# Both MLP products of a hybrid encoder layer as seven block products of halves, with the blocks of u kept in DRAM

## The chip, the cores and the metric

One Trainium2 chip; the kernel runs on one of its cores. The metric is the device time of one launch in microseconds (us). Three runs of the kernel before are shown; their median is 2542.11 us.

## The reference, cut to what matters

One encoder layer over 1024 tokens of 1024 channels in float32: a token mixer of three branches, then an MLP. The change is in the MLP alone (between the norms, D_MODEL = 1024, D_FF = 4096):

```python
def squared_relu_mlp(h, w_up, w_down):
    return jnp.square(jax.nn.relu(h @ w_up)) @ w_down
# out = x1 + rmsnorm(squared_relu_mlp(rmsnorm(x1) * ln_mlp_pre, w_up, w_down)) * ln_mlp_post
```

## The kernel before

The parts follow one another: the input norm, the projections and mixers, the out projection (`out_proj`, from L1037), the MLP (`mlp`, from L1124). A scheduler orders the instructions of all engines by their priority, which is the order in the code; `high_priority` moves loads and casts ahead by a number of instructions, and every wait is put in by it. Tiles come from pools with a fixed number of buffers; a tile waits until the one that had its place is given back.

Every large product is made of three matmuls. An operand is split into hi (rounded to the format that TensorE takes in one pass, an ACT cast, L160) and lo (the rest, a DVE subtraction, L161); `product` (L183 to L190) adds the stationary hi with the moving hi (L188), the stationary hi with the moving lo (L189), and the stationary lo with the moving hi (L190), for every slice k of 128 of the contracted dimension. Each matmul has 128 x 128 stationary and up to 512 moving columns and adds into one bank (128 x 512) of PSUM.

In `out_proj` the 8 token tiles are lifted, multiplied (24 matmuls for each of two banks), normed, and turned by transposes into h (`h_hi`, `h_lo`: channels on the partitions, all 1024 tokens). Its weights, 8 pairs of hi and lo tiles, are held to the end; 12 of those 16 tiles are in the pool `w` of 15 tiles of 128 x 1024, from which the MLP takes its weights too.

The MLP works in 16 blocks of 256 hidden channels. `ups` (L1133) makes u = relu(h w_up)^2 of a block, for each half of the tokens and each 128 channels: 8 slices x 3 matmuls into a bank, relu on ACT (L1142), the square on DVE (L1143), and the split into `uh` and `ul`. `downs` (L1156) multiplies the u of a block with its rows of w_down: 8 token tiles x 2 halves of the output channels, 6 matmuls each, and adds the bank into `acc` in SBUF on DVE (L1164). The order is ups(b+1), then downs(b). The last two blocks are taken together by `finish` (L1166), which also norms a token tile (L1175 to L1182), adds x1 and stores it (L1183). Weights are loaded by the SP queue (L174), 512 KB each. GpSimd (POOL) does a few memsets in the mixers and issues no transfer.

```python
def product(self, bank, stat, mov, close=True, opened=False):            # L183
    for k in range(n):
        (sh, sl), (mh, ml) = stat[k], mov[k]
        mm(bank, sh, mh, start=(k == 0 and not opened), stop=False)      # L188
        mm(bank, sh, ml, start=False, stop=False)                        # L189
        mm(bank, sl, mh, start=False, stop=(close and k == n - 1))       # L190
```

Of the kernel before, what the change touches and what calls it, by code (L numbers as in the profile page):

```python
# [9 lines left out]
F32 = mybir.dt.float32  # L10
# [11 lines left out]
NK = 8  # L22
# [4 lines left out]
LEVELS = (0, 1, 2, 4, 8, 16)  # L27

# [32 lines left out]
def layout(inputs):  # L61
    """The inputs as the kernel reads them: moved, sliced, repeated or padded with zeros, never changed."""
    f = {k: np.asarray(v) for k, v in inputs.items()}
    w = f["w_in"][0]
# [18 lines left out]
    for n, h in enumerate(LEVELS[2:]):  # L83
# [14 lines left out]
        "wup": np.stack([tiled(f["w_up"][0][:, c:c + 256]) for c in range(0, 4096, 256)]),  # L98
        "wdown": np.stack([tiled(f["w_down"][0][c:c + 256]) for c in range(0, 4096, 256)]),
# [14 lines left out]
class Pipe:  # L114
    """What all the parts share: the pools, the constants, the ways to project and to normalise."""

    def __init__(self, ctx, tc, a, out):
        self.tc, self.nc, self.a, self.out = tc, tc.nc, a, out
        pool = lambda name, bufs=1, **k: ctx.enter_context(tc.tile_pool(name=name, bufs=bufs, **k))
        self.const = pool("const")  # L120
        self.hp = pool("h")
        self.wp = pool("w", 15)
        self.dram = pool("scratch", space=DRAM)
        self.pj = pool("pj", 5, space=PSUM)
        self.mx = pool("mx", 3, space=PSUM)
        self.n = 0
        self.ahead = 300
        self.evac = 80
# [29 lines left out]
    def split(self, raw, hi, lo):  # L158
        """raw = hi + lo exactly, both in the format that the tensor engine takes in one pass."""
# [3 lines left out]
    def load_w(self, src, nk, width, late=None):  # L163
        """src [P, nk, width] in DRAM; returns for every k the pair (hi, lo) of [P, width] views."""
# [17 lines left out]
    def product(self, bank, stat, mov, close=True, opened=False):  # L182
        """bank += sum over k of stat[k].T @ mov[k], each a (hi, lo) pair."""  # L183
        mm = self.nc.tensor.matmul
        n = len(stat)
        for k in range(n):
            (sh, sl), (mh, ml) = stat[k], mov[k]
            mm(bank, sh, mh, start=(k == 0 and not opened), stop=False)  # L188
            mm(bank, sh, ml, start=False, stop=False)  # L189
            mm(bank, sl, mh, start=False, stop=(close and k == n - 1))  # L190
# [17 lines left out]
    def rstd(self, ms, eps):  # L208
        """(ms + eps) ** -0.5 for ms, eps [P, 1]: a square root and a reciprocal, and a Newton step on them."""
# [35 lines left out]
def lower_bound(p):  # L245
    """lb = clip(cumsum(softmax(logits, axis=0))[0] - cumsum(...)[0], 0, 1) over the one layer there is."""
# [13 lines left out]
def stage_in(p):  # L260
    """hT = rmsnorm(x) transposed, split: [P, k, T]. A generator: two token tiles a step."""
# [62 lines left out]
def small_part(p):  # L324
    """The 32 narrow columns, B's decay and C's per-token scalars."""
# [91 lines left out]
def conv_silu(p, bank, ct, prev, s):  # L417
    """silu of the causal conv over time of one channel tile, half a sequence; returns (out, padded input)."""
# [15 lines left out]
def keys_part(p, w, pair):  # L434
    """C's keys of two heads: k to DRAM, k k^T with its decay to DRAM, |k|^2."""
# [27 lines left out]
def solve_part(p):  # L463
    """Inverses of the 64 x 64 unit triangles on the diagonal, one per partition (half a, head, chunk).
    A generator: the steps lie between other work."""
# [3 lines left out]
    def turn(x, dst):  # L469
        """x [(a, n), 64] -> dst [(a, m), 64] with dst[a, m, n] = x[a, n, m]."""  # L470
# [162 lines left out]
def decay_part(p, w, pair):  # L633
    """A's decay f = lb + (1 - lb) sigmoid(z) and key k = (1 - lb) sigmoid(-z) of two heads, to DRAM."""
# [66 lines left out]
def token_pairs(p, w):  # L701
    """h @ w (256 columns) two token tiles at a time: yields (t, bank [P, 2, 256])."""
# [7 lines left out]
def first_project(p, w, ready):  # L710
    """A's values of the first group and the 32 narrow columns, tile by tile as the tokens come."""
# [16 lines left out]
def v_project(p, w):  # L728
    """A's or B's values of a group, [tokens, 256], four token tiles per slot."""
# [24 lines left out]
def delta_rule(p, st, q, vv, h, half, o_out, ss_out, sq_out):  # L754
    """One head of C, 512 tokens."""
# [281 lines left out]
def out_proj(p):  # L1037
    """x1 = x + rmsnorm(y @ w_out) * w, and h2 = rmsnorm(x1) * w transposed and split."""
# [12 lines left out]
    def lift(t):  # L1051
        """The tokens of tile t, all channels: transposed and split."""
# [71 lines left out]
def mlp(p, ctx):  # L1124
# [112 lines left out]
```

## Time and profile before

| | |
|---|---|
| runs shown, us | 2533.89, 2542.11, 2547.4 (median 2542.11) |
| span of the profiled execution, us | 2545.3 |
| first and last MLP matmul start, us | 1837.5 and 2537.5 |
| TensorE (PE), VectorE (DVE), ScalarE (ACT) busy | 99%, 55%, 31% |
| mean granted TensorE clock | 0.995 of 2.4 GHz |
| transfers | 200 MB, 79 GB/s in the mean |

The profile is of one execution. Its time beside the span is not given apart from the runs, so the span stands for it: 3.2 us above the median of the runs shown. Times in rows count from the span's start. PE is matmuls, PEld weight loads, which overlap them. A matmul record is longer than the time to the next one, since they are pipelined.

### The profile page before, as it was taken

How to read it: one execution, taken by the hardware profiler on the slowest of the kernel's cores; microseconds unless marked ns; L12 is line 12 of the kernel's file. 1: busy time of each engine (PE TensorE's matmuls, PEld its weight loads, DVE VectorE, ACT ScalarE, POOL GpSimd, SP SyncE). 2: the span in 40 equal slices, each digit the busy share in tenths (PEclk: the TensorE clock that was granted, in tenths of full speed). 3: DMA queues.
4: the chain of work that ended last, by engine and by line, in shares of the span. 5: the costliest groups of instructions: out<-in, count | busy, mean ns of one | idle time of the engine just before them, and what ended most of it. 6: DMA issues, size and time to landing. Idle time of an engine off the chain costs nothing.

```text
span 2545.3 us, 38665 instructions
## 1 busy us (share of the span) xinstructions
PE 2513.0 (99%) x15674; PEld 2202.3 (87%) x15674; DVE 1397.6 (55%) x3125; ACT 776.5 (31%) x1665; POOL 17.8 (1%) x44
## 2 busy tenths in 40 slices
PE   7999999999999999999999999999999999999998
PEld 6788889989888999889899889998788888888887
DVE  5266699945646436555535464445634545454446
ACT  7743434222323122232222232223442121222212
POOL 0000000000000000000000000000000000000000
PEclk9899999999999999999999999999999999999999
DMA  4455512322211122112222111224321111111113
GB/s 149 134 176 158 187 42 88 104 85 72 79 38 50 45 88 78 49 50 76 59 78 61 38 59 59 85 68 130 127 65 51 42 50 50 50 50 50 50 50 124
DMA packets 125234, 200.20 MB, mean 79 GB/s; under 512 B 36592, under 2 KB 66544, under 8 KB 124928
## 3 DMA queue, kind: packets, MB, share of 16 engines
q1 hardware_dynamic: 114688, 178.86, 22.5%
q10 hardware_dynamic: 10368, 18.88, 2.0%
q8 instruction: 123, 2.02, 0.3%
q14 instruction: 55, 0.45, 0.1%
HBM read 156.73 MB, written 40.96 MB: 78 GB/s over the span
## 4 chain that ended last, share of the span: by engine, by line
PE 92%; DVE 3%; DMA 2%; ACT 2%; issue 1%; SPq 0%; DVEq 0%; ACTq 0%
PE pj L188 21%; PE pj L190 21%; PE pj L189 21%; PE dn L188 4%; PE dn L190 4%; PE dn L189 4%; PE L L577 3%; PE Sd L604 1%; PE o L608 1%; PE o L610 1%; DMA wraw<-in_w_dram 1%; PE L L569 1%; PE dS L821 1%; PE vS L817 1%; PE E L553 1%
## 5 line engine op out<-in xcount | busy, mean ns | idle before, releaser
L188 PE MATMUL pj<-whi,hT_hi 128*128 128x256 f32 (+1 forms) x2048 | 587.3, 287 | 5.9 <-ACT hT_hi L294 5.2
L189 PE MATMUL pj<-wlo,hT_hi 128*128 128x256 f32 (+1 forms) x2048 | 586.5, 287 | 0.0
L190 PE MATMUL pj<-whi,hT_lo 128*128 128x256 f32 (+1 forms) x2048 | 586.4, 287 | 0.0
L188 PEld LDWEIGHTS pj<-whi,hT_hi 128*128 128x128 f32 x2048 | 393.3, 192 | 8.3 <-ACT hT_hi L294 6.2
L189 PEld LDWEIGHTS pj<-wlo,hT_hi 128*128 128x128 f32 x2048 | 393.1, 192 | 1.0
L190 PEld LDWEIGHTS pj<-whi,hT_lo 128*128 128x128 f32 x2048 | 392.7, 192 | 0.5 <-DVE hT_lo L295 0.2
L161 DVE TENSOR_TENSOR wlo<-wraw,whi 128x1024 fp32r<-128x1024 f32 (+1 forms) x185 | 225.3, 1218 | 228.3 <-ACT whi L160 207.6
L160 ACT CAST whi<-wraw 128x1024 fp32r<-128x1024 f32 (+1 forms) x185 | 193.5, 1046 | 507.9 <-DMA wraw<-in_wdown_dram 282.3
L190 PE MATMUL pj<-hT_hi,wlo 128*128 128x512 f32 x768 | 310.6, 404 | 0.0
L188 PE MATMUL pj<-hT_hi,whi 128*128 128x512 f32 x768 | 309.9, 404 | 0.0
L189 PE MATMUL pj<-hT_lo,whi 128*128 128x512 f32 x768 | 309.7, 403 | 0.0
L188 PE MATMUL pj<-h_hi,whi 128*128 128x512 f32 x512 | 199.3, 390 | 0.5 <-ACT h_hi L160 0.5
L190 PE MATMUL dn<-whi,ul 128*128 128x512 f32 x512 | 199.3, 389 | 0.0
L189 PE MATMUL dn<-wlo,uh 128*128 128x512 f32 x512 | 199.3, 389 | 0.0
L188 PE MATMUL dn<-whi,uh 128*128 128x512 f32 x512 | 199.2, 389 | 0.0
L189 PE MATMUL pj<-h_lo,whi 128*128 128x512 f32 x512 | 199.2, 389 | 0.0
L190 PE MATMUL pj<-h_hi,wlo 128*128 128x512 f32 x512 | 199.1, 389 | 0.0
L1164 DVE TENSOR_TENSOR acc<-acc,dn 128x512 f32<-128x512 f32 x208 | 141.7, 687 | 99.5 <-PE dn L190 99.4
L190 PEld LDWEIGHTS pj<-hT_hi,wlo 128*128 128x128 f32 x768 | 146.2, 190 | 31.0 <-issue 4.5
L189 PEld LDWEIGHTS pj<-hT_lo,whi 128*128 128x128 f32 x768 | 146.3, 190 | 27.5 <-issue 1.5
L188 PEld LDWEIGHTS pj<-hT_hi,whi 128*128 128x128 f32 x768 | 146.2, 190 | 27.3 <-issue 0.9
L1143 DVE TENSOR_TENSOR relu<-relu 128x512 f32<-128x512 f32 x64 | 44.2, 692 | 148.4 <-ACT relu L1142 148.3
(280 smaller groups left out, 3586.0 us busy)
## 6 DMA issues: line engine op xcount, KB each, us to landing
wraw<-in_w_dram SPq DMA_DIRECT2D x110, 512.0 KB, 3.8
wraw<-in_wup_dram SPq DMA_DIRECT2D x32, 512.0 KB, 4.3
wraw<-in_wdown_dram SPq DMA_DIRECT2D x32, 512.0 KB, 3.8
dt_in<-dt SPq DMA_DIRECT2D x32, 256.0 KB, 3.2
x_in<-in_x_dram SPq DMA_DIRECT2D x8, 512.0 KB, 5.6
browb<-brow SPq DMA_DIRECT2D x16, 256.0 KB, 4.9
fa<-f ACTq DMA_DIRECT2D x16, 256.0 KB, 3.8
ka<-k ACTq DMA_DIRECT2D x16, 256.0 KB, 3.9
```

The costliest lines, as they stand in the source:

```text
L160: self.nc.scalar.copy(hi, raw)
L161: self.nc.vector.tensor_tensor(lo, raw, hi, ALU.subtract)
L188: mm(bank, sh, mh, start=(k == 0 and not opened), stop=False)
L189: mm(bank, sh, ml, start=False, stop=False)
L190: mm(bank, sl, mh, start=False, stop=(close and k == n - 1))
L553: mm(b[:, c, 0:64], k3[:, c, :], q3[:, c, 0:128:2], start=True, stop=True)
L569: mm(b[:, c, :], k3[:, c, :], qx[:, c * P:(c + 1) * P], start=True, stop=True)
L577: mm(b[:, c, 0:64], k3[:, c, :], qb[:, c, :, 1, :], start=True, stop=True)
L604: mm(sb[:, j, :], kt[:, c * P:(c + 1) * P], v_at(half * 4 + c), start=True, stop=True)
L608: mm(ob[:, j, :], at3[:, c, :], v_at(half * 4 + c), start=True, stop=not begun)
L1143: v.tensor_tensor(r, r, r, ALU.mult)
L1164: v.tensor_tensor(dst, dst, bk, ALU.add)
```

## The change

w_up and h are cut in halves along their dimensions, and so are u and w_down. A product of two such 2 x 2 block matrices is then made with Strassen's seven block products (Winograd's form) where eight stood. The sums of blocks that this needs (S1 to S4 on the stationary side, T1 to T4 on the moving side) are made on DVE and split into hi and lo again.

The first product runs over 16 steps m; a step takes 128 channels of each half of the hidden width. Steps 0 and 1 are plain (eight products); between their two halves of the tokens T1 to T4 are formed from h (`combine`). Steps 2 to 15 use seven. They collect in three banks: X takes A11 B11, then on top of it S2 T2, S3 T3 and A22 T4; Z takes S1 T1 and S4 B22; Y takes A12 B21. The partial sums are copied out between. Relu and square of the four blocks are both on ACT. `spread` forms S1 to S4 of u and stores seven blocks of 256 KB a step to DRAM, by the POOL queue.

The second product has seven series over the 16 steps; each loads one 256 KB block of u (SP queue) and, in four of them, one of w_down (SP or POOL queue), makes the sum on the moving side, splits both, and runs 12 matmuls into four banks. All pools of the MLP are new: 26 weight tiles and 14 u tiles of 128 x 512 for the first product; for the second a pool on the memory of h and of T1 to T3. Before, the pools `w`, `h` and the banks were open throughout; now `w` closes with the mixers' pools and the banks' pools close after `out_proj`.

```diff
-        self.wp = pool("w", 15)
+        self.hp = self.hold.enter_context(tc.tile_pool(name="h", bufs=1, side="right"))
...
+    def product(self, bank, stat, mov, close=True, opened=False, more=False):
+            self.nc.tensor.matmul(bank, x, y, start=first and not (opened or more), stop=last and close, skip_group_check=more)
...
+WTILES, UTILES, PLAIN = 26, 14, 2
+    def combine(k):
+        r = {}
+        for n in ("11", "12", "21", "22"):
+            r[n] = ut("r" + n)
+            add(r[n], B[n][0][:, k, :], B[n][1][:, k, :])
+        sub(r["11"], r["12"], r["11"])
+        sub(r["12"], r["22"], r["12"])
+        sub(r["22"], r["22"], r["11"])
+        sub(r["21"], r["21"], r["22"])
+        for n, x in (("T1", "11"), ("T3", "12"), ("T2", "22")):
+            p.split(r[x], T[n][0][:, k, :], T[n][1][:, k, :])
+        return r["21"]
...
+    def keep(n, m, t):
+        ud[n, m] = p.scratch("ud", [P, 512])
+        nc.gpsimd.dma_start(ud[n, m], t)
...
+    def load_up(m):
+        with p.tc.high_priority(offset=p.ahead):
...
+    def up_fast(m, raw):
+        with p.tc.high_priority(offset=p.ahead // 2):
+            h11 = halves(a11)
...
+        p.product(X, stat(h11), mov(B["11"]))
+        act.copy(q1, X)
+        p.product(Z, stat(hs1), mov(T["T1"]))
+        act.copy(q5, Z)
+        p.product(X, stat(hs2), mov(T["T2"]), more=True)
+        act.copy(u2, X)
+        p.product(Z, stat(hs4), mov(B["22"]), more=True)
+        add(u2, Z, u2)
+        p.product(X, stat(hs3), mov(T["T3"]), more=True)
+        act.copy(u3, X)
+        p.product(Y, stat(h12), mov(B["21"]))
+        add(q1, Y, q1)
+        p.product(X, stat(h22), mov(T["T4"]), more=True)
+        add(q5, u3, q5)
+        act.activation(u3, X, AF.Relu)
+        act.activation(u3, u3, AF.Square)
+        for t in (q1, u2, q5):
+            squared(t)
+        spread(m, (q1, u2, u3, q5))
...
+    def step(an, bn, kk):
+        with p.tc.high_priority(offset=p.ahead):
+            u = wt("uin")
+            nc.sync.dma_start(u, ud[an, kk])
+        with p.tc.high_priority(offset=p.ahead // 2):
+            return halves(u), halves(operand(bn, kk))
...
+    series(X, "A11", "B11", False)
+    series(Z, "S1", "T1", False, 0, each(lambda tt: act.copy(q1[tt], X[tt])))
+    series(X, "S2", "T2", True, 0, each(lambda tt: act.copy(q5[tt], Z[tt])))
+    series(Z, "S4", "B22", True, 0, each(lambda tt: act.copy(u2[tt], X[tt])))
+    series(X, "S3", "T3", True, 0, each(lambda tt: add(u2[tt], Z[tt], u2[tt])))
+    series(Y, "A12", "B21", False, 0, each(third))
+    series(X, "A22", "T4", True, 4, {2 + 2 * tt: high(tt) for tt in range(4)})
+    for tt in range(4):
+        partial(4 + tt, X[tt], hs, 0)
+        finish(4 + tt, [X[tt], q5[tt]], x1, hs, 1)
```

In `finish` each token tile of the lower half has a square with its sum on ACT, six small DVE operations, two multiplications and two additions of 128 x 512 on DVE, and two stores.

## Rows read from the trace of the kernel before

**Rows 1.** The page's first part (busy time, share of the span, instructions) and the clock line of its second (granted clock in 40 slices, tenths).

```profile
PE 2513.0 (99%) x15674; PEld 2202.3 (87%) x15674; DVE 1397.6 (55%) x3125; ACT 776.5 (31%) x1665; POOL 17.8 (1%) x44
PEclk9899999999999999999999999999999999999999
```

**Rows 2.** Busy time by stretches, here the middle of the MLP: stretch, its length, busy us and instructions of each engine, granted clock, share of the DMA engines, GB/s.

```profile
core 0: us, PE busy (x) PEld busy (x) DVE busy (x) ACT busy (x) POOL busy (x), PEclk, DMA share, GB/s
1910.00:2470.00 560.00, 560.00 (x2473) 463.92 (x2472) 268.49 (x361) 115.42 (x156) 0.00 (x0) 1.00 0.14 48
```

**Rows 3.** Groups by line: line, engine, operation, tiles, shape, count, then busy us and mean ns of one, then idle time before them. Whole span; the three rows of matmuls with `yh` and `yl` are of the out projection alone (1742 to 1830 us); the last row, of the tile `x_in`, has min, median and max ns instead of the mean.

```profile
L188 PE MATMUL pj<-h_hi,whi 128*128 128x512 f32 x512 | 199.3, 390 | 0.5 <-ACT h_hi L160 0.5
L188 PE MATMUL dn<-whi,uh 128*128 128x512 f32 x512 | 199.2, 389 | 0.0
L161 DVE TENSOR_TENSOR wlo<-wraw,whi 128x1024 fp32r<-128x1024 f32 (+1 forms) x185 | 225.3, 1218 | 228.3 <-ACT whi L160 207.6 <-PE dn L189 16.8 <-PE o L608 2.6
L161 DVE TENSOR_TENSOR ul<-relu,uh 128x512 fp32r<-128x512 f32 x64 | 44.2, 691 | 33.2 <-ACT uh L160 33.1
L1143 DVE TENSOR_TENSOR relu<-relu 128x512 f32<-128x512 f32 x64 | 44.2, 692 | 148.4 <-ACT relu L1142 148.3
L160 ACT CAST uh<-relu 128x512 fp32r<-128x512 f32 x64 | 39.6, 619 | 36.0 <-DVE relu L1143 36.0
L1142 ACT ACTIVATE relu<-pj 128x512 f32<-128x512 f32 x64 | 38.2, 598 | 167.0 <-PE pj L190 167.0
L1164 DVE TENSOR_TENSOR acc<-acc,dn 128x512 f32<-128x512 f32 x208 | 141.7, 687 | 99.5 <-PE dn L190 99.4
...
L188 PE MATMUL pj<-whi,yh 128*128 128x512 f32 x111 | 45.3, 409 | 0.0
L189 PE MATMUL pj<-wlo,yh 128*128 128x512 f32 x111 | 45.1, 407 | 0.0
L190 PE MATMUL pj<-whi,yl 128*128 128x512 f32 x112 | 44.7, 401 | 0.0
...
L281 DVE TENSOR_SCALAR x_in<-x_in,rq_h x8: 747/754/756, 6.9 to 37.7; 128x1024 f32<-128x1024 f32 x8
```

**Rows 4.** The end of the out projection and the start of the MLP, from the timeline (start us, us, engine, line, operation; in brackets the idle time before and what ended it): the first weight load on SP's queue, PE, DVE, and two relus of ACT. The last line is the busy time of the instructions on tiles `pj` in the stretch, in the columns of rows 2 without POOL.

```profile
1826.73 0.33 SPq L174 DMA_DIRECT2D wraw<-in_wup_dram  x1
...
1837.51 0.48 PE L188 MATMUL pj<-h_hi,whi 128*128 128x512 f32 x1
1839.81 0.66 PE L1103 MATMUL h2T<-cs,mixed 128*128 128x128 f32 x4 [1.36 <-DVE h_lo L161]
1852.14 0.96 PE L188 MATMUL pj<-h_hi,whi 128*128 128x512 f32 x3 [0.48 <-ACT h_hi L160]
...
1843.22 1.40 DVE L1089 SCALAR_TENSOR_TENSOR mixed<-pj,rq_h,lnrow 128x512 f32<-128x512 f32 x2
1852.78 1.28 DVE L161 TENSOR_TENSOR h_lo<-h2T,h_hi 128x512 fp32r<-128x512 f32 x2
1853.97 1.28 DVE L1143 TENSOR_TENSOR relu<-relu 128x512 f32<-128x512 f32 x2
...
1852.46 1.10 ACT L1142 ACTIVATE relu<-pj 128x512 f32<-128x512 f32 x2
...
1837.40:1854.10 16.70, 13.88 (x57) 10.41 (x58) 1.40 (x2) 1.78 (x4) 1.00 0.40 142
```

**Rows 5.** Issues of transfers: from where to where, queue, count, KB each, median us from issue to landing. The last line is the duration of SP's own issue instruction (min, median, max ns).

```profile
wraw<-in_wup_dram SPq DMA_DIRECT2D x32, 512.0 KB, 4.3
dt<-browb ACTq DMA_DIRECT2D x16, 256.0 KB, 3.1
fa<-f ACTq DMA_DIRECT2D x16, 256.0 KB, 3.8
out_dram<-z SPq DMA_DIRECT2D x16, 256.0 KB, 2.1
...
L1183 SPq DMA_DIRECT2D out_dram<-z x16: 332/332/337, 2503.3 to 2542.3; - x16
```

**Rows 6.** The end of the kernel, timeline: the last matmul, then ACT's and DVE's last operations. The span ends at 2545.3.

```profile
2537.50 0.39 PE L190 MATMUL dn<-whi,ul 128*128 128x512 f32 x1
...
2538.25 0.15 DVE L1177 TENSOR_SCALAR ms_f<-ms_f 128x1 f32<-128x1 f32 x1
2539.03 0.63 ACT L1175 ACTIVATE relu<-acc 128x512 f32<-128x512 f32 x1 [0.81 <-DVE acc L1173]
2539.79 0.29 ACT L212 ACTIVATE rq_y<-ms_f 128x1 f32<-128x1 f32 x1
2540.11 0.16 DVE L214 RECIPROCAL rq_y<-rq_y 128x1 f32<-128x1 f32 x1
2540.89 1.42 DVE L1182 SCALAR_TENSOR_TENSOR z<-z,rq_h,x1r 128x512 f32<-128x512 f32 x2
```

**Rows 7.** Busy time by stretches, columns as in rows 2: three early stretches and one in the out projection.

```profile
60.00:80.00 20.00, 20.00 (x38) 9.74 (x38) 1.23 (x1) 14.81 (x28) 0.00 (x0) 0.59 0.01 3
80.00:100.00 20.00, 20.00 (x83) 16.23 (x82) 7.14 (x17) 19.80 (x29) 1.05 (x2) 0.90 0.19 57
100.00:120.00 20.00, 20.00 (x137) 18.63 (x136) 10.23 (x30) 14.31 (x23) 0.00 (x0) 1.00 0.79 265
1740.00:1760.00 20.00, 20.00 (x95) 16.11 (x96) 9.81 (x24) 9.20 (x19) 0.00 (x0) 1.00 0.42 143
```

More of the change, by code (lines that the diff above doesn't have):

```diff
@@ new lines, in mlp, with cached @@
+    raws = [load_up(m) for m in range(PLAIN)]
+    raw = load_up(PLAIN)
+    up_plain(range(PLAIN), raws)
+    for m in range(PLAIN, 16):
+        ahead = load_up(m + 1) if m < 15 else None
+        up_fast(m, raw)
+        raw = ahead
+    comb.close()
+    p.hold.close()
+    upper.close()
+    right = ExitStack()
+    dp = right.enter_context(p.tc.tile_pool(name="dw", bufs=1, side="right", reuse_waits="tile"))
+    def cached(n, kk):
+        return dp.tile([P, 512], F32, name=p.name(n), tag=f"{n}{kk}")
@@ new lines, in step, with tiles, series @@
+    def step(an, bn, kk):
+        with p.tc.high_priority(offset=p.ahead):
+            u = wt("uin")
+            nc.sync.dma_start(u, ud[an, kk])
+        with p.tc.high_priority(offset=p.ahead // 2):
+            return halves(u), halves(operand(bn, kk))
+    def tiles(u, tt):
+        return [(u[0][:, tt * P:(tt + 1) * P], u[1][:, tt * P:(tt + 1) * P])]
+    def series(banks, an, bn, more, last=0, between={}):
+        held = []
+        for kk in range(16):
+            if kk in between:
+                between[kk]()
+            u, w = step(an, bn, kk)
+            if kk >= 16 - last:
+                held.append((u, w))
+                continue
+            for tt in range(4):
+                p.product(banks[tt], tiles(u, tt), [w], opened=kk > 0, more=more, close=kk == 15)
+        for tt in range(4 if last else 0):
+            for i, (u, w) in enumerate(held):
+                p.product(banks[tt], tiles(u, tt), [w], opened=True, more=more, close=i == last - 1)
@@ new lines, in acc, with partial, spare, finish @@
+    def acc(s):
+        return [dp.tile([P, 512], F32, name=f"{s}_{tt}") for tt in range(4)]
+    def partial(t, z, ms, c):
+        act.activation(spare(t, 2), z, AF.Square, scale=D ** -0.5, accum_out=ms[:, c:c + 1])
+    def spare(t, i):
+        return cached("c", t % 4 * 4 + i)
+    def finish(t, zs, x1, ms, first):
+        v.tensor_scalar(ms[:, 2:3], ms[:, first:first + 1], EPS, None, ALU.add)
+        r = p.rstd(ms[:, 1 - first:2 - first], ms[:, 2:3])
+        for c in (first, 1 - first):
+            s = slice(c * 512, (c + 1) * 512)
+            o = spare(t, 3) if t > 3 and c != first else zs[c]
+            v.scalar_tensor_tensor(o, zs[c], r, row[:, s], ALU.mult, ALU.mult)
+            v.tensor_tensor(o, o, x1[c], ALU.add)
+            nc.sync.dma_start(p.out[t * P:(t + 1) * P, s], o)
@@ new lines, in residual, with each @@
+    def residual(t):
+        x1 = [spare(t, c) for c in range(2)]
+        for c in range(2):
+            nc.gpsimd.dma_start(x1[c], p.x1d[t][:, c * 512:(c + 1) * 512])
+        return x1
+    X, Z = [bank() for _ in range(4)], [bank() for _ in range(4)]
+    q1, q5, u2, u3 = (acc(n) for n in ("q1", "q5", "u2", "u3"))
+    row = dp.tile([P, 1024], F32, name="row3")
+    nc.gpsimd.dma_start(row, p.a["lnrow"][2])
+    def each(fn):
+        return {2 + 2 * tt: (lambda tt=tt: fn(tt)) for tt in range(4)}
@@ new lines, in mlp, with third @@
+    series(X, "A11", "B11", False)
[3 more added lines that the diff above has]
+    series(X, "S3", "T3", True, 0, each(lambda tt: add(u2[tt], Z[tt], u2[tt])))
+    Y = [bank() for _ in range(4)]
+    def third(tt):
+        act.copy(u3[tt], X[tt])
+        add(q5[tt], u3[tt], q5[tt])
+    series(Y, "A12", "B21", False, 0, each(third))
@@ new lines, in mlp, with high, run @@
+    for tt in range(4):
+        add(q1[tt], Y[tt], q1[tt])
+    low = []
+    def high(tt):
+        def run():
+            ms, hs = p.tiny("ms_f", 3), p.tiny("ms_g", 3)
+            partial(tt, u2[tt], ms, 1)
+            partial(tt, q1[tt], ms, 0)
+            finish(tt, [q1[tt], u2[tt]], residual(tt), ms, 1)
+            partial(4 + tt, q5[tt], hs, 1)
+            low.append((hs, residual(4 + tt)))
+        return run
+    series(X, "A22", "T4", True, 4, {2 + 2 * tt: high(tt) for tt in range(4)})
@@ L1196, in hybrid_encoder_kernel @@
+    for tt in range(4):
+        hs, x1 = low[tt]
+        partial(4 + tt, X[tt], hs, 0)
+        finish(4 + tt, [X[tt], q5[tt]], x1, hs, 1)
+    right.close()
+    left.close()
 @with_exitstack
```

205 lines of the change are left out of this document (131 added, 74 removed).

## The prediction

> **What bounds the kernel now.** I read the page's totals first, then the clock line, then the busy table by stretches of the MLP, then the groups by line, and last the timelines of the MLP's two ends. The totals show TensorE (PE) busy for 99% of the span while VectorE (DVE) has 55% and ScalarE (ACT) 31% [rows 1]: only less matmul time can shorten such a program, unless an engine that is idle now becomes the limit. A busy PE alone need not be a PE at its best, so the stretch table comes next. From 1910 to 2470 us, the middle of the MLP, 2473 matmuls pass in 560 us of unbroken work at the full granted clock (1.00, the 2.4 GHz level) [rows 2]: 226.4 ns from one 512-column matmul to the next, while a single record says 389 [rows 3], because neighbours overlap. The MLP has 1536 matmuls in each of its two products. Their first starts at 1837.5 us [rows 4] and their last ends at 2537.9 [rows 6]: 700 us for 3072, of which 3072 x 0.2264 = 695.5 are matmul time. So the MLP is bound by the number of matmuls, and by nothing else.
>
> **The change part by part.** Everything ahead of the MLP stays in its order; only pools move.
>
> *Matmuls removed.* A hidden step now holds 256 channels, half from each half of the hidden width. The first two steps keep eight block products (96 matmuls each), the other 14 take seven (7 x 4 x 3 = 84): 14 x 12 = 168 fewer. The second product has 7 x 16 x 4 x 3 = 1344 instead of 1536: 192 fewer. 360 x 0.2264 = **-81.5 us**. The operand shapes stay 128x128 and 128x512, so I keep 226.4 ns. The out projection before it runs such matmuls at 401 to 409 ns a record [rows 3] instead of 389; were the excess of some 13 ns by the mean to hold for a third of the 2712 that remain, it would be +12 us, so zero to 12, and I take 0, since the nearest rows are the MLP's own.
>
> *The start.* Today weights for the first step lie ready before the out projection ends: a load is issued at 1826.7 and PE goes from the last projection matmul into the MLP with waits of 1.36 and 0.48 us [rows 4]. The new pools lie on the memory of pools that are closed there, so a load waits until an old tile is given back. Half of the output weights have had their last use 24 matmuls before the end, some 5.5 us ahead, enough for one load (4.3 us median [rows 5]). Behind a load that waits on SP's queue stand the out projection's own last x loads and x1 stores, so a long wait there would delay h too. The new bank pool takes over the old pools' eight banks; the last projection's two are read until 1844.6 [rows 4], and the three of the transposes are in use to the end of h, so three are left to begin with. Bounds: 0, and 12.9 us if no MLP matmul could run before the last h_lo is there (1854.1), because 57 x 0.2264 of them fill the time from 1837.4 now [rows 4]. I take a value near the first end, since the load fits: **+3**.
>
> *The four T operands.* 44 DVE operations (8 additions and subtractions and 3 lo parts for each of 4 slices) and 12 ACT casts. Two DVE operations in a row take 1.28 us, so one costs 0.59 after the other [rows 4]: 26 us. They need h of all tokens (1854.1), except 8 additions. PE has two plain steps meanwhile, 192 x 0.2264 = 43.5 us, and wants T1 at about 1887: 36 x 0.6 = 22 us after 1854.1, plus the weights' lo parts, fits. Were that cover gone, PE would wait the rest. Bounds 0 and 10 us: **+2**.
>
> *A step with seven products.* PE: 84 x 0.2264 = 19.0 us. ACT: 7 casts, 4 bank copies, 8 relu and square passes, 19 operations of at most 0.62 us [rows 3], 11.8 us. DVE: 4 weight combinations, 7 lo parts, 3 bank sums, 4 sums of u, 18 of at most 0.69 us, 12.4 us. Both fit beside PE, so their cost is nothing as long as PE is the slowest. But bank X collects four products in turn and Z two: the third, fourth, fifth and seventh product may begin only when ACT has copied the bank, or DVE drawn on the copy that frees it. Each time one product (12 matmuls, 2.72 us) runs in between, against a copy of 0.59 us. Behind a late copy the whole PE queue stands. Bounds: 0, and 37 us (second rival). I take 0.3 us a step, 14 x 0.3: **+4**.
>
> *Blocks of u in DRAM.* 16 x 7 stores of 256 KB, from POOL's queue, and as many loads from SP's. A store holds nothing up while the 14 tiles of the pool suffice; a step needs 8 of them; behind a late store stand only later stores and, much later, weight loads. SP issues one in 0.33 us and 256 KB land in a median of 2.1 to 3.8 us [rows 5]. At two loads per 2.72 us SP is not full. POOL issues no transfer in this trace, its 44 instructions are memsets [rows 1], so its price is bounded by SP's 0.33 us below and by one transfer at a time, 3.8 us, above (the slowest median of a 256 KB store [rows 5]). Nearest is an issue beside running transfers, hence 0 for the sum; the upper end is the first rival.
>
> Here the trace meets a rule. A DVE operation that takes one input stream runs 1024 columns in 754 ns, the two-input form takes 1218 for 1024 and 691 for 512 [rows 3]: the first has a faster mode, the second passes one column in 1.03 ns. DVE's new MLP work is nearly all of the two-input form. The Trainium skill, "SBUF — State Buffer", section "SBUF: two separate sides" with its note on DVE blocking DMA, says that GpSimd can't write descriptors while DVE runs in a faster two-port mode, so that transfers issued from POOL stand still; its section "A bandwidth-pool intuition that's wrong" gives 3.1 us for one that alone takes 0.62. With 3.1 us a store, an estimate from that page, the sum would be 14 x (7 x 3.1 - 19.0) = 38 us worse; by the rows, where the mode is absent from the two-input form, 0.
>
> *The turn to the second product.* Its cached weights lie on the memory of h and of the T operands, so the first weight block waits for their last uses, perhaps for the last matmul: a load (3.8 us at most in the medians of [rows 5]), a cast (0.62) and a lo part (0.69) make 5.1 us, and 0 if the tile lies where a T operand was. Should PE's clock fall there, at 1.2 GHz, matmuls take twice as long for a while: from 60 to 80 us of this trace, with 38 instructions, it was granted 0.59, back at 1.00 after 100 [rows 7]; 10 us of that add 5. Bounds 0 and 10: **+3**.
>
> *The steps of the second product.* PE 12 x 0.2264 = 2.72 us; ACT two casts, 1.24; DVE two lo parts and at most one combination, 2.1. They fit. Transfers: 512 KB per step where both operands are loaded, 193 GB/s, in four of seven series; 265 GB/s went through from 100 to 120 us [rows 7]. 0.
>
> *The end.* From the last matmul to the span's end are now 7.4 us [rows 6]. In the new tail each of four tiles costs DVE six small operations (1.1 us) and four wide ones (2.7), 3.8 us by the like of them [rows 6], while PE hands one over each 2.72. The first is ready 8.15 - 0.8 us before PE's end, four take 15.2, the last store 3.0: 10.9 us. Bounds 1 and 6: **+3.5**.
>
> Sum: -81.5 + 3 + 2 + 4 + 3 + 3.5 = -66.0. The profiled execution spans 2545.3 us, so 2479.3; the median of the runs shown, 2542.1, is 3.2 us below that span, and I predict for it: 2542.1 - 66.0 = **2476**.
>
> **Rivals.** *POOL's queue becomes the bound (the slower side).* If a store occupies POOL for T us, a step lasts 7T once that exceeds 19.0. With 66 us in hand it gets slower than before above 7T = 19.0 + 66/14, T = 3.4 us; at 3.8, one at a time [rows 5], 14 x (26.6 - 19.0) = 106 us: 2582. For it: no row shows POOL issuing. Against: SP's and ACT's queues have several under way. 9%, two thirds of it on the slower side. The page's 3.1 us would make it 2514.
>
> *A burst on ACT once a step.* At a step's end 8 relu and square passes and the next step's 7 casts may stand ahead of the copy that frees X. 15 x 0.5 (the pitch: two relus in 1.10 us [rows 4]) + 0.6 = 8.1 us; the copy is due after two products, 5.44: 2.7 late, 14 times, 37 us: **2513**. For it: the casts are given precedence by the scheduler. Against: ACT has a third of its time free, and 5 of the 8 passes are ready before the step ends. 12%.
>
> *The second product starves.* If the transfers got only the 143 GB/s of the out projection's time [rows 7], a step with two loads would last 3.67 us: 64 x 0.95 = 61 us, 2537, no change. The 265 GB/s speak against. 5%.
>
> That the products are not seven can't be: the loops are written out.
>
> **How the numbers follow.** Forecast 74%. No wait at all gives 2460.6, less a little for the spread of runs: 2457. Upwards the range takes in the ends of the start (9.9 more) and the turn (7 more), or the burst (2513) with some of them: 2520. About 0.5% (12.7 us) is what a measurement of this kernel can tell from no change. Faster: 74 + 12 + 3 = 89%; same 5%; slower 6%.
>
> **What would show it.** In the changed profile: 2712 MLP matmuls at 226 ns from one to the next; PE idle of a few us near 1840 and at the turn only; X's copies without a queue ahead; stores landing within 4 us; ACT and DVE near 60% in the first product. It is wrong if PE stands at each product of a step, if POOL shows gaps between issue and landing of over 10 us, or if the pitch of the matmuls grows.

## The result: slower by 1.2%, and where 100 us went

| | median of runs, us | ratio to the kernel before, 95% interval | out projection's last matmul to the end, profiled execution |
|---|---|---|---|
| before (four runs; 2542.1 for the three shown ahead) | 2544.8 | | 2545.3 - 1836.1 = 709.2 |
| changed | 2568.4 | 1.0116 [1.0085, 1.0147] | 2564.1 - 1834.2 = 729.9 |
| predicted | 2476 (2457 to 2520) | | 643 |

The third column is used below beside the median. Executions differ by up to 24 us in when the out projection ends (1824.6 to 1848.1 in the profiled ones here), so a stretch that begins there compares MLP with MLP. It leaves out a smaller loss ahead of the MLP: from the 601st matmul, past the first 120 to 130 us, in which executions differ most, to the out projection's last, the kernel before takes 1707.8 us and the changed one 1714.6 in the profiled executions, though both run the same matmuls there. Runs 8 to 13 come back to it.

The page's totals and clock line of the changed kernel, against [rows 1]:

```profile
PE 2464.8 (96%) x15314; PEld 2142.5 (84%) x15314; DVE 1473.0 (57%) x3325; ACT 937.9 (37%) x2003; POOL 114.0 (4%) x221
PEclk9999999999999999999999999999999999799998
```

Exactly 360 matmuls are gone and PE is busy 48 us less. Yet PE now idles 4% of the span, and the clock line has a 7 where the second product begins. The stretches of the MLP, columns as in [rows 2]:

```profile
core 0: us, PE busy (x) PEld busy (x) DVE busy (x) ACT busy (x) POOL busy (x), PEclk, DMA share, GB/s
1920.00:2150.00 230.00, 230.00 (x983) 184.73 (x982) 140.57 (x219) 134.43 (x228) 44.78 (x83) 1.00 0.41 147
...
2178.00:2190.00 12.00, 0.73 (x2) 0.30 (x2) 0.69 (x1) 0.50 (x1) 4.77 (x9) 0.65 0.96 338
2190.00:2210.00 20.00, 6.46 (x16) 4.47 (x17) 13.43 (x21) 5.69 (x10) 9.95 (x19) 0.59 1.04 389
...
2250.00:2490.00 240.00, 226.44 (x965) 184.63 (x964) 131.72 (x213) 99.60 (x184) 13.15 (x24) 0.97 0.37 111
2490.00:2548.00 58.00, 50.27 (x192) 39.12 (x192) 41.76 (x85) 25.62 (x57) 4.38 (x8) 0.89 0.42 137
```

The first row shows the seven-product steps without a gap, but 983 matmuls in 230 us are one per 234.0 ns, where [rows 2] had 226.4. Then come 32 us with 18 matmuls while the transfers run at 338 and 389 GB/s; then series 2 to 6 with small gaps; then series 7 with more. I cut the matmul sequence at its known counts (192 plain, 14 x 84, 7 x 192) and took n x 0.2264 from each piece; the rest is what the change lost:

| piece | time over n x 0.2264 | the prediction's term |
|---|---|---|
| out projection's last matmul to the MLP's first | 14.4 (1.5 before): +12.9 | start +3 |
| plain steps and first fast step (T operands) | 2.4 + 7.1 | T operands +2 |
| fast steps 2 to 13 | 12 x 0.7, all of it distance between matmuls | hand-overs +4, distance 0 |
| last fast step, series 1 | 2.7 + 30.6 | turn +3 |
| series 2 to 6; series 7 | 19.8; 15.0 | steps of the second product 0 |
| last matmul to the end | 15.9 (7.4 before): +8.5 | end +3.5 |

With 4.9 of the same kind in the MLP before, the sum is -81.5 + 12.9 + 86.0 - 4.9 + 8.5 = +21.0; measured 729.9 - 709.2 = +20.7.

**The start**, against [rows 4], PE and DVE:

```profile
1836.57 0.66 PE L1110 MATMUL h2T<-cs,mixed 128*128 128x128 f32 x4 [0.67 <-DVE h_lo L164]
1847.01 1.94 PE L1110 MATMUL h2T<-cs,mixed 128*128 128x128 f32 x8 [9.78 <-DVE mixed L1103]
1848.60 0.77 PE L191 MATMUL ps<-h_hi,whi 128*128 128x512 f32 x1
...
1843.39 0.16 DVE L221 RECIPROCAL rq_y<-rq_y 128x1 f32<-128x1 f32 x1
1843.49 0.69 DVE L164 TENSOR_TENSOR wlo<-uraw,whi 128x512 fp32r<-128x512 f32 x1
1844.10 0.15 DVE L222 TENSOR_TENSOR rq_t<-rq_y 128x1 f32<-128x1 f32 x1
```

In the kernel before, MLP matmuls stood ahead of the last transposes and covered the wait for h. Here none does, and the chain that ends in `mixed` has lo parts of weights between its steps.

**The turn.** SP's and POOL's queues, DVE and PE around the start of series 1, from the timeline (start us, us, engine, line, operation; in brackets idle time before and what ended it):

```profile
2143.58 0.33 SPq L1339 DMA_DIRECT2D uin<-ud  x1
2170.87 15.66 SPq L1304 DMA_DIRECT2D a<-in_wdown_dram  x14
2187.45 0.33 SPq L1339 DMA_DIRECT2D uin<-ud  x1
...
2187.40 4.34 POOL L1304 DMA_DIRECT2D b<-in_wdown_dram  x8 [2.57 <-issue]
...
2190.64 0.69 DVE L1163 TENSOR_TENSOR b<-b,a 128x512 f32<-128x512 f32 x1 [11.92 <-DMA b<-in_wdown_dram]
2191.25 0.68 DVE L164 TENSOR_TENSOR wlo<-a,whi 128x512 fp32r<-128x512 f32 x1
...
2191.99 0.79 PE L191 MATMUL ps<-wlo,whi 128*128 128x512 f32 x1 [12.70 <-DVE wlo L164]
2208.72 0.80 PE L191 MATMUL ps<-wlo,whi 128*128 128x512 f32 x1 [9.60 <-DVE wlo L164]
```

The memory of h and T comes free in the last step of the first product, and everything the scheduler had given precedence rushes in: 48 loads of weights, issued from 2170.87 to 2215.67. On SP 14 `a` loads stand ahead of the second block of u; POOL adds T1's and T2's loads; and DVE, in order, waits 11.92 us for a `b` that only series 2 needs, with the lo part that series 1 needs right behind.

**A boundary between series.** ACT, then PE, at the end of series 1:

```profile
2237.69 0.62 ACT L163 CAST whi<-a 128x512 fp32r<-128x512 f32 x1
2249.49 1.56 ACT L1396 COPY q<-ps 128x512 f32<-128x512 f32 x3 [11.18 <-PE ps L191]
2250.93 0.64 ACT L163 CAST whi<-uin 128x512 fp32r<-128x512 f32 x1
...
2252.63 1.57 PE L191 MATMUL ps<-whi,whi 128*128 128x512 f32 x4 [1.81 <-ACT whi L163]
```

ACT had run 12 us ahead, then stood 11.18 us at three copies of banks that PE had not finished, with series 2's first cast behind them. Its lead was gone when PE needed it: 1.81 us, and then 7 matmuls at 427 ns (the 1.2 GHz level). The gap recurs at all six boundaries, 1.8 to 3.1 us long; a run of 7 to 11 matmuls at 427 ns follows it at four of them.

**The end.** The last matmul, ACT's four passes over the banks, DVE's last operation, against [rows 6]:

```profile
2547.81 0.39 PE L191 MATMUL ps<-whi,wlo 128*128 128x512 f32 x1
2546.88 0.60 ACT L1366 ACTIVATE c<-ps 128x512 f32<-128x512 f32 x1 [2.37 <-PE ps L191]
2547.47 0.59 ACT L1366 ACTIVATE c<-ps 128x512 f32<-128x512 f32 x1
2548.22 0.59 ACT L1366 ACTIVATE c<-ps 128x512 f32<-128x512 f32 x1
2548.98 0.59 ACT L1366 ACTIVATE c<-ps 128x512 f32<-128x512 f32 x1
...
2560.27 0.68 DVE L1379 TENSOR_TENSOR c<-c,c 128x512 f32<-128x512 f32 x1
```

The program holds back the last four hidden steps so that a tile closes every 2.7 us; the scheduler took them step by step again, all four banks closed within 2.1 us, and DVE worked them off alone.

### The profile page after: what moved, and what is told of

Same layout as the page of the kernel before. It is cut to its first block, busy times and chain, and to the rows that moved or that the text cites. A ratio compares the mean times of both kernels' runs of the same rounds, so it can differ in the third digit from the quotient of the medians.

```text
span 2564.1 us, 39624 instructions
## 1 busy us (share of the span) xinstructions
PE 2464.8 (96%) x15314; PEld 2142.5 (84%) x15314; DVE 1473.0 (57%) x3325; ACT 937.9 (37%) x2003; POOL 114.0 (4%) x221
## 4 chain that ended last, share of the span: by engine, by line
PE 80%; issue 10%; DVE 3%; DMA 3%; POOL 2%; ACT 1%; SPq 0%; POOLq 0%; DVEq 0%; ACTq 0%
PE pj L191 51%; PE ps L191 13%; PE L L584 3%; POOL ud L1201 2%; PE Sd L611 1%; PE o L615 1%; PE o L617 1%; PE L L576 1%; PE dS L828 1%; PE vS L824 1%; PE E L560 1%; PE vS L821 1%; DMA b<-in_wdown_dram 1%; PE oc L829 1%; DMA x_in<-in_x_dram 1%
## 5 line engine op out<-in xcount | busy, mean ns | idle before, releaser
L164 DVE TENSOR_TENSOR wlo<-wraw,whi 128x1024 fp32r<-128x1024 f32 (+2 forms) x121 | 147.0, 1215 | 159.3 <-ACT whi L163 156.1
L163 ACT CAST whi<-wraw 128x1024 fp32r<-128x1024 f32 (+2 forms) x121 | 126.3, 1045 | 213.9 <-DMA wraw<-in_w_dram 101.7
L191 PE MATMUL ps<-wlo,whi 128*128 128x512 f32 x448 | 181.1, 404 | 22.3 <-DVE wlo L164 22.3
L191 PE MATMUL ps<-whi,wlo 128*128 128x512 f32 x448 | 180.6, 403 | 0.0
L191 PE MATMUL ps<-whi,whi 128*128 128x512 f32 x448 | 126.4, 403 | 25.1 <-ACT whi L163 25.1
L164 DVE TENSOR_TENSOR wlo<-uin,whi 128x512 fp32r<-128x512 f32 x112 | 77.0, 688 | 99.5 <-ACT whi L163 99.4
L191 PEld LDWEIGHTS ps<-whi,whi 128*128 128x128 f32 x448 | 85.9, 194 | 48.4 <-ACT whi L163 30.9
L191 PEld LDWEIGHTS ps<-wlo,whi 128*128 128x128 f32 x448 | 87.9, 196 | 42.8 <-DVE wlo L164 23.8
L848 ACT ACTIVATE gs<-pj 128x256 f32<-128x256 f32 x96 | 37.0, 386 | 226.8 <-PE pj L191 223.6
L191 PE MATMUL ps<-h_hi,whi 128*128 128x512 f32 x288 | 115.5, 401 | 3.3 <-ACT whi L163 3.3
```

What stands on the lines that cost most here:

```text
L163: self.nc.scalar.copy(hi, raw)
L164: self.nc.vector.tensor_tensor(lo, raw, hi, ALU.subtract)
L191: self.nc.tensor.matmul(bank, x, y, start=first and not (opened or more), stop=last and close, skip_group_check=more)
L848: act.activation(sg[:, :, 0:128], b[:, :, 0:128], AF.Silu)
```

## The experiments

`issue_after(x)` queues what it holds behind x on x's engine: an order of issue, no wait for x to end. Theory: the saved matmuls are lost to orders in in-order queues, and to the matmuls' distance. Rivals: bandwidth, POOL's stores, reading u back.

**1 and 2, the turn.** Run 1 has the `a` loads behind their step's u, run 2 all weight loads, on SP:

```
-            nc.sync.dma_start(u, ud[an, kk])
+            uin[0] = nc.sync.dma_start(u, ud[an, kk]).ins
...
-            (nc.sync if kh + nh == 0 else nc.gpsimd).dma_start(t, p.a["wdown"][kk, :, kh, nh, :])
+            with p.tc.issue_after(uin[0]):
+                nc.sync.dma_start(t, p.a["wdown"][kk, :, kh, nh, :])    # run 1: SP or POOL as before
```

> Only the order of SP's queue at the turn is changed: the load of block B11 of a step is queued behind that step's load of u, instead of 16 of them ahead of the second load of u. The loads for T1 and T2 stay on POOL's queue and all start at the turn, and VectorE's queue may keep its T1 subtractions ahead of the lo parts of the first series. My theory (in-order queues at the turn): the second gap of series 1 (9.6 us, u late) goes, the first (12.7 us, VectorE waits for T1's loads) stays: series 1 about 64 us instead of 74.1, the run about 2558. Rival (the transfers' bandwidth alone limits the turn): the same bytes are wanted at the same time, series 1 stays above 71 us, the run within 3 us of 2568.

> All loads of the second product's weights stand on SP's queue, each behind the load of u of its own step, so that none of T1's and T2's 32 loads starts at the turn. My theory (the turn is lost to 48 loads that start at once and to VectorE waiting in order for loads that series 2 needs): series 1 falls from 74.1 to 46 to 50 us, series 2 and 3 stay at 47, the run 2540 to 2545. Rival (bandwidth: a step with two loads starves): series 1 stays above 60 us, or series 2 and 3 lengthen by over 5 us each, and the run stays above 2560. Rival (reading u back takes too long): gaps stay wherever a u block is read, series 1 above 60 us.

Run 1: 2557.5 us, 1.0064 [1.0036, 1.0091], series 1 60.5 us. Run 2: 2545.3, 1.0019 [1.0000, 1.0038], stretch 702.2, series 1 46.2, series 2 and 3 unchanged at 47.3 and 47.2. The turn in run 2:

```profile
2174.00:2222.00 48.00, 45.83 (x201) 37.27 (x199) 23.93 (x36) 22.36 (x38) 3.77 (x7) 1.00 0.78 258
```

The same bytes, spread by the pace of u's tiles, go at 258 GB/s with PE fed. Bandwidth and read-back fall as causes; 28 us were a matter of queues alone: the same 64 loads of weights, in another order and all on SP's.

**3, copies behind casts.**

```
-            if kk in between:
-                between[kk]()
             u, w = step(an, bn, kk)
+            if kk in between:                    # kk = 4, 6, 8, 10, not 2, 4, 6, 8; in series 7 at 2, 4, 6, 8,
+                                                     # with the sums of Y, which stood ahead of that series
+                with p.tc.issue_after(p.cast), p.tc.issue_after(p.sub):
+                    between[kk]()
```

> In the second product the copies and sums that take a finished series out of its banks are queued on ScalarE and VectorE behind the casts and lo parts of step 4, 6, 8 and 10 of the series after it, instead of where the scheduler had them, ahead of the first casts of the next series. Nothing else is changed. My theory: the gap of 1.8 to 3.1 us at the start of series 2 to 6 and the slow-clock matmuls behind it go: 47.5 us a series becomes 44 to 44.5, 5 x 3.2 = 16 us; series 7 loses some of its 15 too; series 1 stays near 74: the run 2545 to 2553. Rival (the gaps come from u or weight blocks that arrive late): the gaps stay, the run within 4 us of 2568.

2558.2 us, 1.0059 [1.0037, 1.0081]. Series 2 to 6 in one row, then ACT and SP in series 7:

```profile
2250.00:2460.00 210.00, 210.00 (x928) 173.91 (x927) 123.17 (x193) 95.23 (x170) 13.11 (x24) 1.00 0.42 127
...
2475.76 0.62 ACT L163 CAST whi<-uin 128x512 fp32r<-128x512 f32 x1 [3.32 <-DMA uin<-ud]
...
2472.35 0.34 SPq L1381 DMA_DIRECT2D out_dram<-u  x1
2472.79 0.37 SPq L1339 DMA_DIRECT2D uin<-ud  x1
```

No gap is left in series 2 to 6: 43.5 us each instead of 47.0 to 48.4. The expected run time was missed because series 7 went from 58.4 to 66.0: a load of u stands on SP right behind an output store that waits for DVE, and those stores now came later.

**4, stores off SP.**

```
-            nc.sync.dma_start(p.out[t * P:(t + 1) * P, s], o)
+            (nc.gpsimd if t < 4 else nc.sync).dma_start(p.out[t * P:(t + 1) * P, s], o)
```

> Only the output stores of the first four token tiles move, from SP's queue to POOL's, so that series 7's loads of u no longer stand behind stores that wait for VectorE. My theory: series 7 falls from 58.4 us to 50 to 54 (VectorE's 47 us of work in that series stay, and the order of ScalarE's and VectorE's queues); all else unchanged, the run 2560 to 2564. Rival (series 7 is slow only because VectorE is full): series 7 stays at 57 to 60 us and the run within 3 us of 2568.

Series 7: 53.8 us, as expected; the stretch 726.3, 3.6 less. The run was expected at 2560 to 2564 and came at 2571.7, 1.0111 [1.0088, 1.0134]: a gain of 3.6 us does not show in it.

**5, the orders together.** Runs 2 to 4; T4 in place in series 6; and the held products chained (p.mm is the last matmul issued):

```
             load_w(b21[kk], kk, 1, 0)
+            sub(c12[kk], b21[kk], c12[kk])      # T4; series 7 reads c12
...
+                with p.tc.issue_after(p.mm):
                     p.product(banks[tt], tiles(u, tt), [w], opened=True, ...)
```

> The paced loads (all on SP, each behind its step's u), the bank copies behind the casts, and the stores on POOL together; with them series 7's operand T4 is subtracted in place already in series 6, and the last four hidden steps of series 7 are kept tile by tile on TensorE's queue, so that the banks of the four upper tiles close one after the other instead of all within 2.2 us. My theory (the saving is real and was lost to in-order queues): series 1 46 us, series 2 to 6 43.5 each, series 7 44 to 47, from the last matmul to the end 9 to 12 us instead of 15.9: 2568 - 28 - 19 - 13 - 5 = 2503, between 2498 and 2510, faster than the kernel before by 1.3 to 1.8%. Rival (something shared, bandwidth or ScalarE, limits the second product): the gaps come back elsewhere, a series stays above 46 us on the mean, the run above 2520.

2504.0 us, 0.9844 [0.9824, 0.9864]; stretch 663.4; series 45.6, 5 x 43.5, 45.6; last matmul to the end 9.7. 66 us of the stretch came back with the same products and the same transfers: by the order of queues, 48 loads of weights and eight stores on another queue, and one operand subtracted a series earlier. That operand and the chained products were tried only together with the rest, so their shares of the 66 us are not known.

**6 and 7, h at the low end; the start.** Run 6 adds to run 5 an exchange of the sides of all pools but the constants'; run 7 also queues DVE's lo parts of the first up weights behind the residual chain of the last token tile (p.last):

```
+    tc.swap_default_side()       # and side="left" for h, comb and dw
...
-        w = [[halves(x) for x in raw] for raw in raws]
+        with p.tc.issue_after(p.last):
+            w = [[halves(x) for x in raw] for raw in raws]
```

> The kernel of the run with the five orders, and the two ends of SBUF exchanged: h (with the T operands, later the cached weights) at the low end, as in the kernel before, the other pools at the high end. Nothing else differs. If the place of h sets the distance between matmuls that stream it: 226.7 instead of 234.3 ns in the MLP's first product, 1368 x 7.6 ns = 10.4 us, and 3 to 6 us in the mixers: 13 to 17 us less than the run with the five orders, about 2488. If the distance is set by what else goes on in the first product: the same time within 4 us. A third way: the pool that now lies high is the one of the weights, which every product reads as its other operand; then the second product would get the longer distance, 1344 x 7.6 ns, and nothing is gained.

> As the run with h at the low end, and VectorE's lo parts of the first up weights queued behind the last operation of the out projection's residual chain, five of which stood between its steps. My theory: the last transposes of h run some 3 us earlier, the first MLP matmul too (1848.6 by the changed kernel's time, 1845.6 then, counted from the same end of the out projection), and the run gains 2 to 4 us. Rival (the weights' loads, which wait for tiles of the out projection, set the start): no gain.

Run 6: 2493.3 us, but the matmuls' distance in the first product stayed at 233.5 ns and the stretch at 661.5: that theory fell. Most of the run's gain lies ahead of the MLP, in matmuls of another width (runs 8 to 13). Run 7: 2490.0, 0.9784 [0.9761, 0.9808]; the wait of the last transposes of h fell from 9.78 us to

```profile
1836.53 1.94 PE L1110 MATMUL h2T<-cs,mixed 128*128 128x128 f32 x8 [7.06 <-DVE mixed L1103]
```

**8 to 13, the matmuls' distance.** The edits move pools only, and the order of the work stays: the kernel before with `side="right"` for h's pool; the kernel before with a 32-byte pool between h and the rest; the changed kernel with 32, 416 and 160 bytes above h; the kernel of run 7 with 32 bytes.

```
-        self.hp = pool("h")
+        self.hp = pool("h", side="right")       # before, h high
...
+        self.nc.vector.memset(pool("pad", side="right").tile([P, 104], F32, name="pad"), 0.0)   # ahead of h: 416 bytes; 8 or 40 columns: 32 or 160
```

> The kernel before, with nothing changed but the place of the pool of h: at the high end of SBUF, where the change puts it, instead of the low end. If the place of h sets the distance between matmuls that stream it: about 234 ns instead of 226.7 in the MLP's first product, 1536 x 7.6 ns = 11.7 us, and some us more in the mixers, so 10 to 20 us slower than the kernel before: 2555 to 2565. If the longer distance in the first product comes from the seven products themselves (banks that are left and taken up again, VectorE and ScalarE busier, stores): 226.7 ns stays, and the time is within 4 us of the kernel before.

> The kernel before, with 32 unused bytes a partition between h and the pools above it; the order of all work stays. In the runs so far, wherever h (what the matmul streams) and the weights (what it holds) start at addresses that are equal modulo 64 bytes, matmuls follow each other at 226.7 ns (the kernel before; the second product of every Strassen run), and where they differ by 32 it is 233 to 234 (the Strassen kernel with h at either end, the kernel before with h at the high end). If that is the cause: the MLP's first product goes from 226.7 to 233 to 234 and the run is 13 to 20 us slower than the kernel before, as with h at the high end. If the distance between h and the weights in SBUF, or the end at which one lies, is the cause: nothing changes, within 4 us.

> The changed kernel with 32 unused bytes a partition above h at the high end of SBUF, so that h and the T operands start at multiples of 64 bytes as the weights do; all else, all orders too, stays. By the address theory: 226.7 instead of 234.3 ns in the first product, 10 us, and 4 to 7 us in the mixers: about 2553. By the theory that the ends of SBUF or the work beside it count: 2568, within 4 us.

> The kernel of the run with the start order (five orders, h at the low end), with the same 32 bytes at the high end, ahead of all pools that lie there. By the address theory 13 to 17 us less than without them: about 2475, near the 2476 of the prediction and 2.7% faster than the kernel before. By the other theories: 2490, within 4 us.

> The changed kernel with 416 unused bytes a partition above h at the high end: h and the T operands (what the matmul streams) then start at 64 modulo 512 bytes, as the weights do. In all runs so far, matmuls follow at 226.7 to 227 ns where both operands have the same start modulo 512 (64 and 64, 96 and 96, 480 and 480, 448 and 448) and at 233 to 234 where they differ (480 and 64, 64 and 480, 64 and 96, 448 and 64). By this: 226.7 ns in the first product, 10 us less there, and up to 5 in the mixers: 2553 to 2560. If the equal starts are a coincidence, and the ends of SBUF or the work beside it count: 233 to 234 ns, 2568 within 4 us.

> The same with 160 bytes in place of 416: h starts at 320 modulo 512, the weights at 64, equal modulo 256 but not modulo 512. If 256 bytes are the period that counts: 226.7 ns in the first product and the time of the run with 416 bytes, 2553 to 2560. If 512 are: 233 to 234 ns, 2568 within 4 us.

Starts are bytes in a partition, from the built programs; the distance, the time from one matmul's start to the next, is the mean over neighbouring 512-column matmuls that stream h in the MLP.

| kernel | h, weights | modulo 256 | ns | run |
|---|---|---|---|---|
| before | 25664, 91200 | 64, 64 | 226.7 | |
| before, h high | 163808, 25664 | 224, 64 | 234.2 | 2560.5, 1.0070 [1.0040, 1.0100] |
| before, 32 bytes | 25664, 91232 | 64, 96 | 233.3 | 2547.4, 1.0019 [0.9998, 1.0041] |
| changed | 163808, 28736 | 224, 64 | 234.3 | 2568.4 |
| orders, h low | 25664, 173024 | 64, 224 | 233.5 | 2493.3 |
| changed, 32 bytes | 163776, 28736 | 192, 64 | 233.1 | 2569.1, 1.0099 [1.0069, 1.0129] |
| run 7, 32 bytes | 25664, 172992 | 64, 192 | 233.1 | 2489.0, 0.9800 [0.9764, 0.9836] |
| changed, 416 bytes | 163392, 28736 | 64, 64 | 226.7 | 2560.0, 1.0071 [1.0047, 1.0094] |
| changed, 160 bytes | 163648, 28736 | 64, 64 | 226.7 | 2553.3, 1.0058 [1.0038, 1.0077] |

The same 200 us of the first product, changed kernel with 32 bytes, then with 160:

```profile
1940.00:2140.00 200.00, 200.00 (x859) 160.78 (x858) 119.86 (x187) 115.42 (x196) 37.62 (x70) 1.00 0.41 144
```

```profile
1940.00:2140.00 200.00, 200.00 (x884) 165.62 (x883) 121.92 (x189) 118.18 (x201) 37.60 (x70) 1.00 0.40 142
```

My first two readings (the end of SBUF, equality modulo 64) fell; equality modulo 256 holds in all nine, and in the second products, whose operands have equal starts and pass at 226.7 to 227.1 ns. Two runs that only shift the kernel before show it without any of the change.

The run time of the kernel before with 32 bytes can't be told from that without, although its MLP is 9.1 us longer (709.0 from the first matmul's start to the last one's, 700.0 before). The traces show why: the same bytes made the part ahead of the MLP 8.4 us shorter (1699.4 from the 601st matmul to the out projection's last, 1707.8 before). There 5952 matmuls of 256 columns stream weights past a held tile of the normed input, hT. One of their three groups on the pages, first before, then with 32 bytes (a record overlaps the next one):

```profile
L188 PE MATMUL pj<-whi,hT_hi 128*128 128x256 f32 (+1 forms) x2048 | 587.3, 287 | 5.9 <-ACT hT_hi L294 5.2
```

```profile
L189 PE MATMUL pj<-whi,hT_hi 128*128 128x256 f32 (+1 forms) x2048 | 579.8, 283 | 5.8 <-ACT hT_hi L295 5.5
```

Their mean distance is 119.8 ns before and 116.8 with 32 bytes, so at this width equal starts are not the fast case. It is 119.8 in run 5 and 117.7 in run 6, where the part ahead of the MLP fell from 1713.3 to 1703.0 us: that is most of run 6's gain. The 2304 matmuls of 512 columns that stream hT there go the way of the table: 228.6 ns before and 233.9 in the changed kernel, while the 256-column ones have 119.8 in both. That goes with the 6.8 us that the changed kernel loses ahead of the MLP; with 416 or 160 bytes that part takes 1706.1 and 1705.7 us.

**14, POOL's stores doubled.**

```
         nc.gpsimd.dma_start(ud[n, m], t)
+        nc.gpsimd.dma_start(p.scratch("ud2", [P, 512]), t)
```

> The changed kernel with every store of a block of u issued twice from POOL's queue, the second to a place that nobody reads: 14 stores a step in place of 7. From the changed kernel's trace (0.54 us to issue one, no gap on TensorE in the steps): 7.6 us of POOL in a step of 19.7, nothing changes but the rate of the transfers, some 140 GB/s to 230: the run within 5 us of 2568. By the prediction's rival (a store holds POOL for 3.4 us or more, one after the other): 47 us a step and more, over 350 us slower. In between, if transfers at that rate delay the weights' loads: gaps at the start of steps.

```profile
1940.00:2140.00 200.00, 200.00 (x855) 160.79 (x854) 118.50 (x185) 116.45 (x194) 78.40 (x148) 1.00 0.70 248
```

148 issues in 78.4 us, 0.53 each, and no gap: POOL is not the bound even at twice the load. The run, 2575.8, 1.0127 [1.0094, 1.0159], is 3 us outside the expectation; the pieces that grew by 2 us or more are the first fast step, series 1 and series 7.

**15, all together:** the orders, the start, the 416 bytes.

> The five orders, the start order, h at the high end, and the 416 bytes above it. By the theory of equal starts: from 2503.98 (five orders) less 3 (start) less 10 to 15 (the matmuls' distance): 2486 to 2491 without a gain in the mixers, 2480 with all of it. With no effect of the starts: about 2500.

2488.0 us, 0.9780 [0.9752, 0.9808], stretch 649.3: 59.9 us less than before, 80.6 less than the change.

```profile
1925.00:2150.00 225.00, 225.00 (x994) 186.03 (x993) 140.13 (x218) 134.65 (x229) 45.67 (x85) 1.00 0.42 147
2172.00:2216.00 44.00, 43.68 (x193) 35.99 (x193) 27.70 (x42) 22.17 (x37) 1.62 (x3) 1.00 0.77 259
2216.00:2434.00 218.00, 218.00 (x963) 180.59 (x962) 145.64 (x231) 101.84 (x180) 4.39 (x8) 1.00 0.52 159
2434.00:2479.00 45.00, 43.62 (x191) 35.33 (x189) 38.75 (x91) 24.20 (x59) 8.65 (x16) 1.00 0.52 170
```

What stays of the loss is the start (11.7 us), the first fast step (7.1), the edges of series 1 and 7, and the end (9.7).

## Why the prediction was wrong, step by step

- **Matmuls removed, -81.5:** right, 360 fewer.
- **A step with seven products, +4:** the hand-overs cost nothing, and the burst on ACT did not come.
- **Blocks of u in DRAM, 0:** right in the steps. A store's issue takes POOL 0.54 us, and these are the changed kernel's transfers, against [rows 5]:

```profile
uin<-ud SPq DMA_DIRECT2D x112, 256.0 KB, 2.7
...
ud<-us POOLq DMA_DIRECT2D x64, 256.0 KB, 2.8
...
ud<-q POOLq DMA_DIRECT2D x28, 256.0 KB, 2.3
```

  The first rival is refuted by run 14. The Trainium skill, "SBUF — State Buffer", sections "SBUF: two separate sides" and "A bandwidth-pool intuition that's wrong", has a transfer issued from POOL take 3.1 us, and 0.62 alone, where DVE's faster mode runs beside it; this trace has 0.54 us for a store's issue and 2.3 to 2.8 to its landing, beside DVE at 61% (140.57 of 230 us), all of it in the two-input form of [rows 3]. No run here puts the faster mode beside POOL's stores.
- **The turn, +3 within 0 to 10:** failed, and the largest single piece: 30.6 us in series 1. I costed one load, one cast and one lo part, as if the first needed block came first. I did not ask what else becomes free to start there (48 loads), nor what stands ahead in SP's and DVE's orders. Runs 1 and 2 show it.
- **The steps of the second product, 0:** failed, and more in sum: 34.8 us (19.8 in series 2 to 6, 15.0 in series 7). Work per step was added up per engine and fits (run 5 shows PE fed at 43.5 us a series); what I left out are the operations between series, which wait for PE and hold ACT, DVE and SP behind them. Runs 3 to 5 show it. The third rival had transfers starving this product; run 2 feeds PE at 258 GB/s, so bandwidth was not what these steps lacked.
- **The start, +3 within 0 to 12.9:** the upper end came, 12.9. Run 7 gives back 2.7 of it; whether the weights' loads set the rest was not tried, so its cause stays open.
- **T operands, +2 within 0 to 10:** 6.5 in the first fast step, a gap of 3.3 us behind ACT's casts and 9 matmuls near 427 ns after it. Not tried apart, so why those casts were late stays open.
- **The end, +3.5 within 1 to 6:** 8.5. I read the order of the last products from the code; the scheduler had another. With it enforced the end is 9.7 us, +2.3.
- **The distance, 0 within 0 to 12:** 10.4 us in the first product (1368 x 7.6 ns), by an address that the view of a timeline does not show. The same address lies behind "only pools move", which put the part ahead of the MLP at 0: it lost 6.8 us.

The sign was lost at the edges: the turn, the boundaries between series and the end were each costed by their first wait or not at all, and none by the queue behind it.

## What to carry to other kernels

A change that lets PE off is worth its matmuls only if every other queue keeps its lead: at each point where memory comes free or a result is handed over, write down the order of each in-order queue, and for each entry that waits, who stands behind it. Read that order from the schedule, not from the program's text. And where two pools feed one matmul, look at where they start, and try it for each shape of matmul: in the kernel before, 32 bytes cost 512-column matmuls 3% of their time and gave 256-column ones 2.5%, and the two cancelled.

## What the runs showed of the hardware

- In the MLP, matmuls of 512 columns follow each other at 226.7 ns when the streamed and the held operand start at the same place modulo 256 bytes, and at 233.1 to 234.3 when they start 32, 128 or 160 bytes apart. Matmuls of 256 columns in the mixers, with weights streamed and hT held, do not follow that rule: 119.8 ns with equal starts (kernel before; 416 and 160 bytes) and also in the changed kernel, 116.8 with 32 bytes in the kernel before, 117.7 in run 6. Why is open; other types were not tried. The Trainium skill, "TensorE: Matmul & The Clock Gate", section "Step-by-step: what each phase is for", has two independent read ports for the two operands; in these runs the time still depends on where one operand lies relative to the other. Its section "Wait — 56ns, not 53.3ns?" gives 215.7 ns from start to start for 512 columns; no stretch here came below 226.
- After gaps of 1.8 to 3.1 us at the boundaries between series PE passed 7 to 11 of its next matmuls at 427 ns (1.2 GHz) in four cases of six; 12 and 20 us with little work show a granted clock of 0.65 and 0.59.
- When 48 loads of weights were issued within 45 us, the transfers ran at 389 GB/s in 20 of those 45 us, and loads of u issued then took 9 to 15 us to land instead of the median of 2.7.
